# One layer of a hybrid mixer, attention and MLP trunk on one core: the mixer's output projection by seven block products, its convolution by three filters, and the memory values placed behind the projection

## The chip, the core and the metric

The kernel runs on one core of a Trainium2 chip. Five engines take part, each with its own queue of instructions: TensorE (PE; its weight loads, PEld, are listed apart), VectorE (DVE), ScalarE (ACT), GpSimd (POOL), and SyncE (SP), which issues all DMA transfers here. The metric is the device time of one execution in microseconds, as a median of several runs.

## What is computed

One layer, x of 1024 positions by 1024 channels in f32, with three sub-layers, each added to x after an RMS norm:

```python
h = rms_norm(x, pre_mix_g); z = h @ w_in + b_in
y_a = pool_mixer(z[:, :256], pool_w, pool_scale)         # trailing-window means
y_b = spatial_gating_mixer(z[:, 256:1024], ...)          # gMLP on blocks of 128 positions
y_c = conformer_conv_mixer(z[:, 1024:], ...)             # GLU, causal conv of 31 taps, LayerNorm, swish
x = x + rms_norm(concat(y_a, y_b, y_c) @ w_out, post_mix_g)
h = rms_norm(x, pre_x_g); m = rms_norm(mem, mem_g)
x = x + rms_norm(memory_cross_attention(h, m, wq, wk, wv, wo), post_x_g)   # 4 heads, 256 memory tokens
h = rms_norm(x, pre_ff_g)
x = x + rms_norm(square(relu(h @ w_ff1)) @ w_ff2, post_ff_g)               # 4096 hidden
```

The convolution is depthwise over 384 channels: `h = conv(a * sigmoid(g)) + conv_b`, then a LayerNorm over the 384 channels of a position, then swish.

## The kernel before

**Products.** An f32 factor is split into a high part in fp32r (`...h`, a cast on ACT) and a low part (`...l`, source less high part, on DVE or POOL). A product of two such factors is three matmuls (`mm3`): high by high, high by low, low by high. Activations are held transposed, channels on the 128 partitions. `seven` (line 955) multiplies two 1024x1024 matrices by seven products of 512x512 blocks instead of eight; each product has four row blocks of four steps of three matmuls. `left_factors` and `right_factors` make its block sums, in tiles of 1024 columns, and their high and low parts. The query projection (pq), the attention's output projection (ox) and both MLP products go by seven blocks already; the mixer's output projection (omp, lines 978 to 995) goes by plain products: eight blocks of 128 positions by two halves of 512 columns, by eight steps of three matmuls. Behind each block `residual` adds it to x and norms it, and PE transposes the result (om0t to om7t) for pq.

**Stages.** Input norm and the products of the convolution's columns (zg, za) give hc, three tiles of 128 channels by 1024 positions. `conv_taps` (line 588) runs 31 taps for each of three tiles and two halves on DVE, each tap an operation of up to 512 columns on an accumulator in PSUM (cacc). Meanwhile PE runs the products of the other columns (zb), block by block, with the gMLP (zz, vl, sv, ybt) and the pooling (zat, ph, pya) behind them, then the memory's transposes (memt), the keys' product (wkp) and the keys' transposes (kt). `conv_norm` (line 604) goes block by block: PE transposes it to positions on partitions (cnat), DVE takes statistics (cst, cmv), POOL a power of -0.5 (cr...r), DVE scales (cn), PE transposes back (cback), ACT takes the sigmoid (csg). The first half's stands ahead of the values' product (wvp, `mem_product("wv")`), the second half's behind it. Keys and values are then parked in DRAM, and the projection follows.

**What sets the order.** `Schedule` records every operation in the order of the program, and `order` (line 229) then places them by list scheduling: it takes the operation with the earliest planned start on any engine, ties by due time, with planned durations (`_cost`, line 203; a transfer counts at 360 GB/s), planned delays between engines, 49 places of 4 KB per partition for tiles and eight banks of PSUM. Due times come from the order in which the program lists the PE operations. A transfer may be issued at most 150 PE operations ahead of its place. All is fixed before the kernel runs: each engine takes its list in order, and waits where an input is late. Every instruction is recorded under one line, 161, so the names of tiles tell them apart.

Of the kernel before, what the change touches and what calls it, by code (L numbers as in the profile page):

```python
# [10 lines left out]
F32 = mybir.dt.float32  # L11
F32R = mybir.dt.float32r
AF = mybir.ActivationFunctionType
ALU = mybir.AluOpType
# [15 lines left out]
NS = 49  # L30
# [35 lines left out]
class Schedule:  # L66
# [15 lines left out]
    SLACK = 50000.0  # L82
    BYDUE = ("act", "dve", "pool", "sync")
# [119 lines left out]
    def _cost(eng, method, args, kw, ins):  # L203
# [3 lines left out]
        if method == "dma_start":  # L207
            return max(450.0, n * args[0].shape[0] * 4 / 360.0)
# [20 lines left out]
    def order(self):  # L229
        ops, tiles, tags = self.ops, self.tiles, self.tags  # L230
        for i, op in enumerate(ops):
# [5 lines left out]
        due, at = [0.0] * len(ops), 0.0  # L237
        for i, op in enumerate(ops):
            if op.eng == "pe":
                at += op.cost  # L240
            due[i] = at + (0.0 if op.eng == "pe" else self.SLACK)
# [128 lines left out]
def block_kernel(ctx: ExitStack, tc: tile.TileContext, x, mem, pre_mix_g, w_in, b_in, pool_w,  # L370
# [22 lines left out]
    def small(name, n, bufs=24):  # L393
        return sc.tile(mp, [P, n], F32, f"m{n}", bufs, name)
# [93 lines left out]
    for k in range(NK):  # L488
        units[f"out{k}"] = row_unit(f"out{k}", w_out, k)
# [70 lines left out]
    hc = [slot(f"hc{j}", [S]) for j in range(3)]  # L560
    for j, hf in ((0, 0), (1, 0), (0, 1), (1, 1), (2, 0), (2, 1)):
# [15 lines left out]
        else:  # L577
# [4 lines left out]
        dve.scalar_tensor_tensor(hc[j][:, hf * H:(hf + 1) * H], pa, bC[:, j:j + 1], sg,  # L582
                                 ALU.add, ALU.mult)


    yt = [[None] * NK, [None] * NK]

    def conv_taps(hf):
        accs = []
        for j in range(3):  # L590
            acc = bank(f"cacc{hf}{j}")
            dve.tensor_scalar(acc, hc[j][:, hf * H:(hf + 1) * H], cw[:, TAPS - 1, j:j + 1],
                              cb[:, j:j + 1], ALU.mult, ALU.add)
            for s in range(1, TAPS):
                k = TAPS - 1 - s
                a0 = s if hf == 0 else 0
                dve.scalar_tensor_tensor(acc[:, a0:H], hc[j][:, hf * H + a0 - s:hf * H + H - s],
                                         cw[:, k, j:j + 1], acc[:, a0:H], ALU.mult, ALU.add)
            cs = slot(f"cs{hf}{j}", [H])
            act.copy(cs, acc)  # L600
            accs.append(cs)
        return accs

    def conv_norm(hf, cs):
        for j in range(3):
            yt[hf][5 + j] = slot(f"yc{hf}{j}", [2, H], F32R)
        back = [bank(f"cback{hf}{j}") for j in range(3)]
        nat = [bank(f"cnat{hf}{i}") for i in range(2)]
        for b in range(4):
            ps = nat[b % 2]  # L610
            for j in range(3):
                pe.transpose(ps[:, j * P:(j + 1) * P], cs[j][:, b * P:(b + 1) * P], ident)
            st = small(f"cst{hf}{b}", 6)
            dve.bn_stats(st, ps[:, :384])
            mv = small(f"cmv{hf}{b}", 2)
            dve.bn_aggr(mv, st)
            r = rstd_of(f"cr{hf}{b}", mv[:, 1:2], 1)
            nt = slot(f"cn{hf}{b}", [384])
            dve.tensor_scalar(nt, ps[:, :384], mv[:, 0:1], r, ALU.subtract, ALU.mult)
            for j in range(3):  # L620
                pe.transpose(back[j][:, b * P:(b + 1) * P], nt[:, j * P:(j + 1) * P], ident)
        for j in range(3):
            sg = slot(f"csg{hf}{j}", [2, H])
            act.activation(sg[:, 0, :], back[j], AF.Sigmoid, scale=clg[:, j:j + 1],
                           bias=clb[:, j:j + 1])
# [770 lines left out]
```

## Time and profile before

| | |
|---|---|
| median of 3 runs | 1198.07 us (1197.9 to 1200.57) |
| the profiled run, and its span | 1196.5 us, 1194.8 us |
| PE busy | 1158.2 us, 97% |
| DVE busy | 875.1 us, 73% |
| ACT busy | 556.2 us, 47% |
| POOL busy | 271.0 us, 23% |
| DMA | 163.11 MB, mean 137 GB/s |

The durations are of one profiled execution. The busy time of PE is that of pipelined matmuls, and a matmul's listed duration includes its time in the pipe: the distance between the starts of two is what one costs. The stages stand in the trace roughly so: input norm to 41 us, convolution's columns and the blocks of the other columns to 192, keys' product to 226, values' product and the mixer's projection with pq to 428, attention to 490, ox to 580, the MLP's first product to 880, its second to 1186.

### The profile page before, as it was taken

The page shows a single profiled execution, that of the slowest core. Times are in us where ns is not written, and L with a number is a line of the kernel's source. Part 1 is how long each engine was busy: PE and PEld are TensorE (multiplying, and loading weights), DVE is VectorE, ACT ScalarE, POOL GpSimd, SP SyncE. Part 2 cuts the span into 40 slices and gives each one's busy share as a digit, 9 for nine tenths or more (in the row PEclk, how much of TensorE's full clock was granted, in tenths as well). Part 3 has the DMA queues.
Part 4 walks back from the last instruction along what each step waited for, and adds up shares of the span by engine and source line. Part 5 has one row for each costly group of instructions (what it writes and reads, how often), then busy time and mean ns, then how long its engine had stood idle before and what let it go on. Part 6 is the DMA issues. An engine that isn't in the chain of part 4 may idle for free.

```text
span 1194.8 us, 14793 instructions
## 1 busy us (share of the span) xinstructions
PE 1158.2 (97%) x5387; PEld 957.9 (80%) x5387; DVE 875.1 (73%) x1234; ACT 556.2 (47%) x973; POOL 271.0 (23%) x260
## 2 busy tenths in 40 slices
PE   7999999999999999999999999999999999999997
PEld 6788877787877898788778878888888888888885
DVE  5899999464459757799996877667589744587736
ACT  6422245734566358749833434333364632435421
POOL 5352458894062403443000000000000000000001
PEclk9999999999999999999999999999999999999999
DMA  8400024652240313126043355444685244443443
GB/s 275 152 1 1 1 91 164 243 207 89 88 159 28 114 53 107 58 101 229 36 159 123 141 192 169 159 149 142 211 301 210 89 141 169 167 168 132 144 156 141
DMA packets 86056, 163.11 MB, mean 137 GB/s; under 512 B 6475, under 2 KB 29919, under 8 KB 85983
## 3 DMA queue, kind: packets, MB, share of 16 engines
q1 hardware_dynamic: 85982, 162.17, 39.1%
q8 instruction: 42, 0.69, 0.2%
q14 instruction: 32, 0.25, 0.1%
HBM read 116.01 MB, written 46.14 MB: 136 GB/s over the span
## 4 chain that ended last, share of the span: by engine, by line
PE 76%; DVE 9%; ACT 6%; DMA 4%; POOL 2%; issue 2%; SPq 1%; DVEq 0%; ACTq 0%; POOLq 0%
PE g L161 25%; PE fx L161 13%; PE fz L161 7%; PE zb L161 5%; PE ox L161 4%; PE omp L161 4%; PE pq L161 4%; PE zg L161 3%; PE za L161 2%; PE fy L161 2%; DVE cacc L161 2%; PE wkp L161 2%; ACT h L161 1%; PE sc L161 1%; ACT junk L161 1%
## 5 line engine op out<-in xcount | busy, mean ns | idle before, releaser
L161 POOL TENSOR_TENSOR fr0r<-fr0e,half 128x1 f32<-128x1 f32 x1 | 0.9, 866 | 590.2 <-DVE fr0e L161 590.2
L161 DVE SCALAR_TENSOR_TENSOR cacc<-hc,taps,cacc 128x512 f32<-128x512 f32 (+14 forms) x180 | 121.0, 738 | 0.2
L161 DVE TENSOR_TENSOR c<-c,fz 128x512 f32<-128x512 f32 x32 | 21.8, 684 | 52.2 <-PE fz L161 34.1
L161 DVE TENSOR_TENSOR acc<-acc,g 128x512 f32<-128x512 f32 x40 | 25.8, 681 | 33.1 <-PE g L161 33.1
L161 ACT COPY c<-fx 128x512 f32<-128x512 f32 x48 | 28.4, 596 | 38.6 <-PE fx L161 29.2
L161 ACT ACTIVATE c<-fx 128x512 f32<-128x512 f32 x16 | 9.6, 598 | 61.0 <-PE fx L161 61.0
L161 ACT CAST w1o<-w1a 128x512 fp32r<-128x512 f32 x32 | 20.3, 638 | 29.4 <-DVE sb L161 7.8
L161 DVE SCALAR_TENSOR_TENSOR c<-c 128x512 f32<-128x512 f32 x48 | 32.5, 684 | 0.3
L161 PE MATMUL sc<-kv,q 128*128 128x256 f32 x192 | 30.3, 291 | 0.0
L161 ACT ACTIVATE junk<-acc 128x512 f32<-128x512 f32 x16 | 10.1, 632 | 40.8 <-DVE acc L161 40.6
L161 PE MATMUL fx<-h3a40h,w1o 128*128 128x512 f32 x64 | 25.4, 397 | 2.2 <-ACT c L161 2.2
L161 PEld LDWEIGHTS sc<-kv,q 128*128 128x128 f32 x192 | 26.0, 190 | 0.9
L161 ACT CAST w1o<-w1c 128x512 fp32r<-128x512 f32 x32 | 19.6, 626 | 14.2 <-PE fz L161 5.3
L161 PE MATMUL o<-pT,kv 128*128 128x512 f32 x96 | 24.9, 394 | 1.4 <-DVE pT L161 1.4
L161 PE MATMUL fx<-h3a60h,w1o 128*128 128x512 f32 x64 | 25.3, 401 | 0.0
L161 PE MATMUL fx<-h3a11h,w1o 128*128 128x512 f32 x64 | 25.2, 393 | 0.0
L161 PE MATMUL fz<-h3a30h,w1o 128*128 128x512 f32 x64 | 25.1, 392 | 0.0
L161 PE MATMUL fy<-h3a21h,w1o 128*128 128x512 f32 x64 | 25.0, 393 | 0.0
L161 PE MATMUL fy<-h3a20h,w1o 128*128 128x512 f32 x64 | 24.9, 390 | 0.0
L161 PE MATMUL fz<-h3a50h,w1o 128*128 128x512 f32 x64 | 24.9, 389 | 0.0
L161 PE MATMUL fx<-h3a41h,w1o 128*128 128x512 f32 x64 | 24.9, 389 | 0.0
L161 PE MATMUL fz<-h3a31h,w1o 128*128 128x512 f32 x64 | 24.9, 389 | 0.0
(1555 smaller groups left out, 3991.5 us busy)
## 6 DMA issues: line engine op xcount, KB each, us to landing
ha<-scr_hid SPq DMA_DIRECT2D x56, 512.0 KB
scr_hid<-c SPq DMA_DIRECT2D x48, 256.0 KB
scr_hid<-sa SPq DMA_DIRECT2D x32, 256.0 KB
scr_hid<-sb SPq DMA_DIRECT2D x32, 256.0 KB
x<-in_x_dram SPq DMA_DIRECT2D x8, 512.0 KB
omx<-in_x_dram SPq DMA_DIRECT2D x8, 512.0 KB
scr_x<-omx SPq DMA_DIRECT2D x8, 512.0 KB
wqb<-in_wq_dram SPq DMA_DIRECT2D x8, 512.0 KB
```

The costliest lines, as they stand in the source:

```text
L161: op.fn = lambda: f(*[put(a) for a in args], **{k: put(v) for k, v in kw.items()})
```

## The change

- **Projection.** `projection` is written once and called for om and for ox. The mixer's projection goes by `seven`: 336 matmuls in place of 384. Its outputs' factors come from `left_factors`, w_out's from `right_factors`, for om both on DVE (ox keeps half of its right factors on POOL). w_out is loaded as 512-column halves (omwb) and no longer as eight rows (out0 to out7) with low parts on POOL. The mixer's outputs y are kept unsplit in f32 (yq), so their low parts (DVE and POOL) go. 12 sums on DVE and 12 copies on ACT take the products.
- **Convolution.** hc is held by even and odd positions, with their sum hs. Three filters (16 even taps, 15 odd, 16 summed) run over 512 columns for each channel tile, both halves of the sequence at once: 141 tap operations in place of 186, and combining operations behind them.
- **Norm.** `conv_norm` goes in pairs of blocks, each block with a bank of its own; csg is 256 wide (24 operations in place of 12). Both halves follow the keys' product at once.
- **Values.** The values' product and the parking stand behind the projection, ahead of pq.
- **POOL** does its 1024-wide differences and low parts in two halves of 512.
- **Planner.** Transfers count at 220 GB/s; six passes are made, each with due times from the PE order of the one before, and the one with the shortest plan is kept; 50 places; 18 small tiles in place of 24.

```diff
-            return max(450.0, n * args[0].shape[0] * 4 / 360.0)
+            return max(450.0, n * args[0].shape[0] * 4 / 220.0)
...
+        for n in range(self.PASSES):
+            out = self._order(pe)
+            self.spans = getattr(self, "spans", []) + [self.span]
+            if best is None or self.span < best[0]:
+                best = (self.span, out, [op.end for op in self.ops],
+                        {k: r["at"] for k, r in self.tiles.items()})
+            pe = [i for i in out if self.ops[i].eng == "pe"]
...
+        for f, src, w, n in (("a", hc[j][:, 0, :], lambda i: cw[:, 30 - 2 * i, j:j + 1], 16),
+                             ("b", hc[j][:, 1, :], lambda i: cw[:, 29 - 2 * i, j:j + 1], 15),
+                             ("c", hs[j], lambda i: cws[:, 15 - i, j:j + 1], 16)):
+            acc = bank(f"cacc{f}{j}")
+            dve.tensor_scalar_mul(acc, src, w(0))
+            for i in range(1, n):
+                dve.scalar_tensor_tensor(acc[:, i:], src[:, :H - i], w(i), acc[:, i:],
+                                         ALU.mult, ALU.add)
+            accs.append(acc)
+        a, b, c = accs
+        ua = slot(f"cua{j}", [H])
+        act.activation(ua, a, AF.Identity, bias=cb[:, j:j + 1])
+        cs = slot(f"cs{j}", [H, 2])
+        act.copy(cs[:, 0:1, 0], ua[:, 0:1])
+        dve.tensor_tensor(cs[:, 1:, 0], ua[:, 1:], b[:, :H - 1], ALU.add)
+        dve.tensor_tensor(ua, ua, b, ALU.add)
+        dve.scalar_tensor_tensor(cs[:, :, 1], c, cb2[:, j:j + 1], ua, ALU.add, ALU.subtract)
...
+        for pr in range(2):
+            back = [bank(f"cback{hf}{pr}{j}")[:, :256 * n].rearrange("p (j n) -> p j n", n=256)
+                    for j, n in ((0, 2), (1, 1))]
+            for i in range(2):
+                b = pr * 2 + i
+                ps = bank(f"cnat{hf}{b}")
...
+    cs = [conv_taps(j) for j in range(3)]
+    conv_norm(0, cs)
+    conv_norm(1, cs)
...
+        for c in range(2) if eng is pool else (slice(0, 2),):
+            lo_of(eng, lo[:, c], src[:, c], hi[:, c])
...
+            if i == 1:
+                act.copy(row[b][:, c0], ps)
+            elif i == 2:
+                dve.tensor_tensor(row[b][:, c0], row[b][:, c0], ps, ALU.add)
...
+        seven(name, left_factors(name, A), right_factors(f"{name}w", w, (dve, dve) if name == "om" else (pool, dve)), take)
...
+    h2 = projection("om", {hf: [yq[hf][0:2], yq[hf][2:4]] for hf in range(2)}, w_out, g_x,
+                    post_mix_g, x, x1d)
+
+    ps = mem_product("wv")
```

Three places in the orders show what moved. The numbers behind a name tell instances of it apart. First PE behind the keys' transposes (kt), where blocks of the convolution go through their norm; before:

```order
L161 MATMUL cnat00_239<-ident_74,cs00_1429 128x128
L161 MATMUL cnat01_240<-ident_74,cs00_1429 128x128
L161 MATMUL cback02_238<-ident_74,cn00_2565 128x128
L161 MATMUL cnat00_239<-ident_74,cs01_1452 128x128
L161 MATMUL cback02_238<-ident_74,cn01_2573 128x128
L161 MATMUL cnat00_239<-ident_74,cs02_1742 128x128
L161 MATMUL cnat01_240<-ident_74,cs01_1452 128x128
L161 MATMUL wvp00_257<-wv0h_2322,mT00_2259 128x512
L161 MATMUL cnat01_240<-ident_74,cs02_1742 128x128
L161 MATMUL wvp00_257<-wv0l_2571,mT00_2259 128x512
```

and now, the last twelve rows ahead of the projection's second matmul:

```order
L162 MATMUL cnat13_286<-ident_74,cs1_1725 128x128
L162 MATMUL cnat13_286<-ident_74,cs2_1760 128x128
L162 MATMUL cback010_255<-ident_74,cn02_2600 128x128 x2
L162 MATMUL cback010_255<-ident_74,cn03_2613 128x128 x2
L162 MATMUL cback011_256<-ident_74,cn02_2600 128x128
L162 MATMUL cback011_256<-ident_74,cn03_2613 128x128
L162 MATMUL cback100_267<-ident_74,cn10_2629 128x128 x2
L162 MATMUL cback101_268<-ident_74,cn10_2629 128x128
L162 MATMUL cback100_267<-ident_74,cn11_2633 128x128
L162 MATMUL cback101_268<-ident_74,cn11_2633 128x128
L162 MATMUL cback100_267<-ident_74,cn11_2633 128x128
L162 MATMUL om10_291<-omww10h_2355,oma10h_2141 128x512
```

Before, the values' matmuls (wvp) stand among the transposes of the norm; now six blocks (cnat02 to cnat13, 18 transposes) and 16 cback transposes stand between the last kt and the first om10, with no product among them.

DVE at the same place, now: the start of the norm of these six blocks, with parts of the projection's factors (oma, omww) and of the keys (kT01) among them.

```order
L162 BN_STATS cst02_258<-cnat02_257 128x6
L162 BN_STATS cst03_263<-cnat03_262 128x6
L162 BN_AGGR cmv02_259<-cst02_258 128x2
L162 TENSOR_TENSOR oma11l_2579<-yq01_1678,oma11h_1938 128x1024
L162 TENSOR_SCALAR cr02e_260<-cmv02_259 128x1
L162 BN_AGGR cmv03_264<-cst03_263 128x2
L162 TENSOR_TENSOR omww20l_2584<-omwb100_2455,omww20h_2483 128x1024
L162 TENSOR_SCALAR cr03e_265<-cmv03_264 128x1
L162 TENSOR_TENSOR kT01_2591<-kt0_230,kT00_2539 128x512
L162 TENSOR_SCALAR cn02_2600<-cnat02_257,cmv02_259,cr02r_261 128x384
L162 BN_STATS cst10_270<-cnat10_269 128x6
L162 BN_STATS cst11_275<-cnat11_274 128x6
```

The chain from cnat to cn has factor parts of 1024 columns in its way, which were no part of the program before; the second half of a2 (oma21l) stands 43 rows behind the first of these, that of a6 (oma61l) 61.

Last, DVE at the start of the MLP's first product, where the left factors of h3 are made (h3a60l is the low part of the first half of factor 6); before:

```order
L161 TENSOR_TENSOR h3a60l_5619<-h3s20_5595,h3a60h_5607 128x1024
L161 TENSOR_TENSOR h3100_5431<-h3000_5165,h3100_5431 128x1024
L161 TENSOR_TENSOR h3a61l_5638<-h3s21_5604,h3a61h_5623 128x1024
L161 TENSOR_TENSOR h3a50l_5649<-h3s10_5575,h3a50h_5591 128x1024
L161 TENSOR_TENSOR w1o05_5562<-w1a0_5238,w1o05_5562 128x512
L161 TENSOR_TENSOR w1b0_5308<-w1d0_5323,w1b0_5308 128x1024
L161 TENSOR_TENSOR h3101_5443<-h3001_5170,h3101_5443 128x1024
L161 TENSOR_TENSOR w1c0_5256<-w1c0_5256,w1t0_5564 128x1024
L161 TENSOR_TENSOR h3a51l_5685<-h3s11_5586,h3a51h_5599 128x1024
L161 TENSOR_TENSOR w1o07_5679<-w1b0_5308,w1o07_5679 128x512
L161 TENSOR_TENSOR h3010_5188<-h3010_5188,h3s20_5595 128x1024
L161 TENSOR_TENSOR h3011_5234<-h3011_5234,h3s21_5604 128x1024
```

and now:

```order
L162 TENSOR_TENSOR h3a60l_5688<-h3s20_5662,h3a60h_5678 128x1024
L162 TENSOR_TENSOR h3a61l_5697<-h3s21_5673,h3a61h_5685 128x1024
L162 TENSOR_TENSOR w1o16_5665<-w1t0_5629,w1o16_5665 128x512
L162 TENSOR_TENSOR oxh100_5509<-oxh000_5239,oxh100_5509 128x1024
L162 TENSOR_TENSOR w1b0_5421<-w1d0_5445,w1b0_5421 128x1024
L162 TENSOR_TENSOR oxh101_5527<-oxh001_5258,oxh101_5527 128x1024
L162 TENSOR_TENSOR h3a70l_5741<-oxh100_5509,h3a70h_5727 128x1024
L162 TENSOR_TENSOR w1o07_5734<-w1b0_5421,w1o07_5734 128x512
L162 TENSOR_TENSOR w1o17_5738<-w1b0_5421,w1o17_5738 128x512
L162 TENSOR_TENSOR w1o05_5651<-w1a0_5318,w1o05_5651 128x512
L162 TENSOR_TENSOR h3a50l_5766<-h3s10_5640,h3a50h_5657 128x1024
```

h3a70l, the low part of the first half of factor 7, stood fourteenth from h3a60l (two rows behind the last one shown); now it is seventh, and factor 5 comes behind it. (The tiles h3... of before are called oxh... now.)

## Rows read from the trace of the kernel before

**Rows 1.** The page's busy time of each engine, with its share of the span and the number of its instructions.

```profile
PE 1158.2 (97%) x5387; PEld 957.9 (80%) x5387; DVE 875.1 (73%) x1234; ACT 556.2 (47%) x973; POOL 271.0 (23%) x260
```

**Rows 2.** Busy time of each engine by stretch. Columns: the stretch, its length, then PE, PEld, DVE, ACT and POOL busy with the count of instructions, the granted clock of PE as a share of full speed, the DMA engines' busy share, GB/s.

```profile
0.00:41.00 41.00, 31.28 (x197) 27.36 (x198) 25.59 (x51) 26.91 (x47) 22.09 (x62) 1.00 0.79 267
...
140.00:192.00 52.00, 48.56 (x238) 39.25 (x237) 49.70 (x103) 24.05 (x43) 33.24 (x37) 0.98 0.34 122
192.00:226.00 34.00, 31.07 (x146) 25.16 (x147) 25.05 (x47) 20.78 (x32) 26.70 (x25) 0.92 0.40 140
226.00:428.00 202.00, 199.13 (x929) 163.92 (x928) 118.90 (x146) 101.60 (x200) 97.97 (x69) 1.00 0.34 120
428.00:490.00 62.00, 59.28 (x381) 52.93 (x380) 48.38 (x91) 48.00 (x114) 15.64 (x6) 1.00 0.23 77
490.00:580.00 90.00, 89.98 (x428) 74.13 (x427) 78.22 (x102) 65.56 (x155) 33.42 (x21) 1.00 0.40 141
580.00:612.00 32.00, 27.93 (x114) 22.07 (x113) 31.59 (x34) 18.02 (x26) 0.00 (x0) 0.95 0.15 49
612.00:880.00 268.00, 265.85 (x1168) 218.28 (x1167) 193.36 (x281) 105.50 (x175) 0.00 (x0) 1.00 0.48 168
880.00:1186.00 306.00, 306.00 (x1351) 253.11 (x1349) 202.95 (x212) 119.73 (x146) 4.77 (x6) 1.00 0.47 163
```

**Rows 3.** Two pieces of the chain of waits that ended last: start, duration, engine, what, number of instructions.

```profile
489.92 50.83 PE ox L161 x224
...
885.55 300.35 PE g L161 x1325
```

**Rows 4.** What PE waited for, over the whole span: the waiting tile, the engine and tile waited for, us in total, times, the longest.

```profile
PE fx L161 <- DVE h3a70l L161: 3.2, 1, 3.2
PE ybt L161 <- DVE zz L161: 2.9, 2, 2.4
PE fx L161 <- ACT c L161: 2.4, 3, 1.5
PE zat L161 <- ACT zt L161: 2.1, 1, 2.1
PE om6t L161 <- DVE omt L161: 1.5, 1, 1.5
PE o L161 <- DVE pT L161: 1.4, 1, 1.4
...
PE pT L161 <- DVE pt L161: 1.3, 1, 1.3
```

**Rows 5.** The stretches before and behind 600 us, for the tiles omp alone; columns are PE, PEld, DVE and ACT, then clock, DMA share and GB/s.

```profile
0.00:600.00 600.00, 91.10 (x384) 71.29 (x384) 10.86 (x16) 10.85 (x32) 0.99 0.32 109
```

**Rows 6.** The convolution's taps in the page's list of groups: busy us and mean ns of one behind the bar.

```profile
L161 DVE SCALAR_TENSOR_TENSOR cacc<-hc,taps,cacc 128x512 f32<-128x512 f32 (+14 forms) x180 | 121.0, 738 | 0.2
```

**Rows 7.** The timeline of DVE in the query projection: start, duration, what. Two low parts of 1024 columns, one behind the other.

```profile
371.39 1.22 DVE L161 TENSOR_TENSOR h2a60l<-h2s,h2a60h 128x1024 fp32r<-128x1024 f32 x1
372.53 1.22 DVE L161 TENSOR_TENSOR h2a61l<-h2s,h2a61h 128x1024 fp32r<-128x1024 f32 x1
```

**Rows 8.** The timeline of DVE behind the keys' product, in the norm of blocks 2 and 3 of the first half (two statistics in one row).

```profile
227.36 1.02 DVE L161 BATCH_NORM_STATS2 cst<-cnat 128x6 f32<-128x384 f32 x2
...
228.38 0.65 DVE L161 TENSOR_TENSOR kT<-kt,kT 128x512 fp32r<-128x512 f32 x1
...
229.76 0.68 DVE L161 TENSOR_SCALAR cn<-cnat,cmv,cr02r 128x384 f32<-128x384 f32 x1 [0.39 <-POOL cr02r L161]
230.35 0.67 DVE L161 TENSOR_SCALAR cn<-cnat,cmv,cr03r 128x384 f32<-128x384 f32 x1
```

**Rows 9.** The timeline of POOL there: the power for block 2.

```profile
229.17 0.55 POOL L161 TENSOR_TENSOR cr02r<-cr02e,half 128x1 f32<-128x1 f32 x1 [0.78 <-DVE cmv L161]
```

**Rows 10.** The timeline of PE there: ten transposes of the keys, and the three transposes back of block 3.

```profile
223.92 1.26 PE L161 MATMUL kt<-ident,kn 128*128 128x128 f32 x10
...
231.33 0.49 PE L161 MATMUL cback<-ident,cn 128*128 128x128 f32 x3
```

**Rows 11.** The timeline of PE some 12 us earlier: a wait of 2.39 us, and two matmuls that follow each other 3 us later.

```profile
212.00 0.41 PE L161 MATMUL ybt<-ident,zz 128*128 128x128 f32 x2 [2.39 <-DVE zz L161]
...
215.26 0.63 PE L161 MATMUL pya<-ph,pw 128*128 128x512 f32 x1
215.68 0.63 PE L161 MATMUL wkp<-wk6h,mT 128*128 128x512 f32 x1
```

**Rows 12.** The timeline of POOL there: the low parts of the keys' last row of weights.

```profile
217.13 2.58 POOL L161 TENSOR_TENSOR wk7l<-wk7r,wk7h 128x512 fp32r<-128x512 f32 x2
```

**Rows 13.** The timeline of DVE in the attention: the scalings of two pairs of blocks.

```profile
469.06 0.61 DVE L161 TENSOR_SCALAR pt<-pt,rs 128x256 f32<-128x256 f32 x2
...
474.70 3.89 DVE L161 TENSOR_SCALAR pt<-pt,rs 128x256 f32<-128x256 f32 x2
```

**Rows 14.** The timeline of POOL there.

```profile
473.57 2.40 POOL L161 TENSOR_TENSOR wob<-wob,wob 128x1024 f32<-128x1024 f32 x1
476.06 2.38 POOL L161 TENSOR_TENSOR wot<-wob,wob 128x1024 f32<-128x1024 f32 x1
```

**Rows 15.** The timeline of DVE at the start of the MLP's first product: the first and the last of the fourteen instructions shown of the order above.

```profile
584.78 1.22 DVE L161 TENSOR_TENSOR h3a60l<-h3s,h3a60h 128x1024 fp32r<-128x1024 f32 x1
...
597.94 1.21 DVE L161 TENSOR_TENSOR h3a70l<-h,h3a70h 128x1024 fp32r<-128x1024 f32 x1
```

More of the change, by code (lines that the diff above doesn't have):

```diff
@@ L229, in order, with _order @@
     def order(self):
+        best, pe = None, [i for i, op in enumerate(self.ops) if op.eng == "pe"]
+        for n in range(self.PASSES):
[5 more added lines that the diff above has]
+            pe = [i for i in out if self.ops[i].eng == "pe"]
+        self.span, out, ends, places = best
+        for op, end in zip(self.ops, ends):
+            op.end = end
+        for k, at in places.items():
+            self.tiles[k]["at"] = at
+        return out
+    def _order(self, pe_order):
         ops, tiles, tags = self.ops, self.tiles, self.tags
+        for op in ops:
+            op.users = []
         for i, op in enumerate(ops):
@@ L234, in order @@
                 ops[d].users.append(i)
-        due, at = [0.0] * len(ops), 0.0
+        for tag in tags.values():
+            tag["free"] = [(0.0, i) for i in range(tag["bufs"])]
+        for r in tiles.values():
+            r.update(left=len(r["ops"]), end=0.0, live=False, at=0)
+        due, at = [None] * len(ops), 0.0
+        for i in pe_order:
+            at += ops[i].cost
+            due[i] = at
+        at = 0.0
         for i, op in enumerate(ops):
             if op.eng == "pe":
-                at += op.cost
-            due[i] = at + (0.0 if op.eng == "pe" else self.SLACK)
+                at = max(at, due[i])
+            else:
+                due[i] = at + self.SLACK
         for i in range(len(ops) - 1, -1, -1):
@@ L391, in bank, with small @@
         return sc.tile(pp, [P, 512], F32, "b", 8, name)
-    def small(name, n, bufs=24):
+    def small(name, n, bufs=18):
         return sc.tile(mp, [P, n], F32, f"m{n}", bufs, name)
@@ L557, in prod_t @@
                 act_h[k][:, 1, c0:c1], k == 0, k == NK - 1)
-    hc = [slot(f"hc{j}", [S]) for j in range(3)]
+    hc = [slot(f"hc{j}", [2, H]) for j in range(3)]
+    hs = [slot(f"hs{j}", [H]) for j in range(3)]
     for j, hf in ((0, 0), (1, 0), (0, 1), (1, 1), (2, 0), (2, 1)):
@@ L604, in conv_norm @@
-    def conv_norm(hf, cs):
[L605 to L610, printed above, removed]
-            for j in range(3):
[L612 to L625, printed above, removed]
-            act.activation(sg[:, 1, :], back[j], AF.Identity, scale=clg[:, j:j + 1],
-                           bias=clb[:, j:j + 1])
-            dve.tensor_tensor(sg[:, 1, :], sg[:, 1, :], sg[:, 0, :], ALU.mult)
-            y = yt[hf][5 + j]
-            act.copy(y[:, 0, :], sg[:, 1, :])
-            lo_of(pool, y[:, 1, :], sg[:, 1, :], y[:, 0, :])
@@ new lines, in block_kernel, with y_of @@
+        dve.tensor_tensor(hs[j][:, c], hc[j][:, 0, c], hc[j][:, 1, c], ALU.add)
+    yq = [[slot(f"yq{hf}{t}", [2, H]) for t in range(4)] for hf in range(2)]
+    def y_of(hf, i):
+        return yq[hf][i // 2][:, i % 2, :]
+    cws = sc.tile(cp, [P, 16, 3], F32, "cws", 1, "cws")
+    dve.tensor_copy(cws[:, 0, :], cw[:, 0, :])
+    dve.tensor_tensor(cws[:, 1:16, :], cw[:, 2:TAPS:2, :], cw[:, 1:TAPS - 1:2, :], ALU.add)
+    cb2 = sc.tile(cp, [P, 3], F32, "cb2", 1, "cb2")
+    dve.tensor_scalar(cb2, cb, 2.0, None, ALU.mult)
@@ L710, in block_kernel @@
             zaT[hf][m] = slot(f"zaT{hf}{m}", [H + 16])
-        for j in range(3):
-            yt[hf][2 + j] = slot(f"yb{hf}{j}", [2, H], F32R)
         for pr in range(2):
@@ L933, in sub @@
             for e in range(2):
[L934 removed]
+                for c in range(2) if eng[e] is pool else (slice(0, 2),):
+                    eng[e].tensor_tensor(o[e][:, c], x[e][:, c], y[e][:, c], ALU.subtract)
         def factor(i):
```

156 lines of the change are left out of this document (67 added, 89 removed).

## The prediction

> **What bounds the kernel now.** I read the busy time of the engines first: TensorE (PE) is busy for 1158.2 of 1194.8 us, and VectorE (DVE) for 875.1 [rows 1]. The table of stretches then shows where PE is not busy [rows 2]: the idle time from 140 to 1186 us is 3.4, 2.9, 2.9, 2.7, 0, 4.1 and 2.2 us by stretch (length less PE's busy time), some 18 us in all; the rest lies in the first 41 us (9.7), which the change hardly touches, and in the last nine. The granted clock is below 1.00 in three of these stretches, and costs at most 0.08 x 34 = 2.7, 0.02 x 52 = 1.0 and 0.05 x 32 = 1.6 us there. In the chain of waits, PE's products run end to end: 224 matmuls in 50.83 us, 1325 in 300.35 us, 0.227 us for each at full clock [rows 3]. So a matmul less is 0.227 us less, and beside that there are some 18 us of idle time and 5 us of clock to win, each with a name in the list of PE's waits [rows 4].
>
> [...]
>
> **The change part by part.** The profiled run took 1196.5 us, 1.6 below the median of 1198.07; the sum is made against it.
>
> 1. The projection's matmuls: 384 now [rows 5], seven products of 4 x 4 x 3 = 336 then; 48 x 0.227 = **-10.9**.
>
> 2. The convolution's normalisation. PE has, so far, matmuls of the values' product to do while a block goes through statistics, power, scaling and back (the order of before shows them interleaved, and the trace shows wvp running with the last two blocks). The values' product is now behind the projection, and the order of after has nothing for PE between the last key transpose and the first om10 but 18 cnat and 16 cback transposes: 34 x 0.109 = 3.7 us [rows 10]. What releases them is DVE: six statistics at 0.47, six aggregates and six small sums (some 0.6 together), four scalings at 0.59, one kT part of 0.6 [rows 8] and the two 1024-wide lo parts that the order puts among them at 1.14 [rows 7], 8.7 us; a power on GpSimd, 0.55 [rows 9], is partly exposed, and the first statistics and the last transposes add 1.5. That is 10.8 us from the last kt to om10, less 3.7 of transposes: 7.1 us of new idle time. After such a wait the clock falls: behind the wait of 2.39 us for zz the matmuls stood 0.42 us apart [rows 11], so I add 1. Bounds: if the blocks interlock better than I count, +3; if the three remaining pairs run one after another (one pair took 4.5 us from its statistics at 227.36 to the last cback at 231.82 [rows 8, 10], so 3 x 4.5, with 3 x 0.65 of transposes ahead and 4 x 1.14 of lo parts between, 20.0 less 3.7) it is 16.3, with 2.7 of clock **+19**. Taken **+8**, nearest to the rows of one pair counted out singly.
>
> 3. The factors of the projection. Left and right factors each add 22 operations of 1024 columns on DVE, 44 x 1.14 = 50 us [rows 7], and 14 casts each on ACT, beside 336 x 0.227 = 76 us of PE. In the stretch from 226 to 428 us DVE was busy for 118.9 of 202 us [rows 2], so there is room in the sum. But they bunch: the first three products (36 us of PE) want a1, a2, a6 and w1, w2, w6, and some of the norm stands ahead of them. By the order, the second half of a2 is some 20 us of DVE work behind the start of the norm and that of a6 some 38 us; PE is there, after the stall of term 2, at about 23 and 37 us. About level: **+1**, bounds 0 and +6 (five 1024-wide operations late).
>
> 4. Behind the projection the values' product (96 matmuls, 22 us) now covers the last blocks' residuals. The wait of om6t for omt, 1.5 us [rows 4], was the largest part of the 2.9 us idle between 226 and 428 us [rows 2]; in the order of after wvp rows lie among om4t to om7t. **-2**, bounds -2.9 and 0. What parks keys and values goes later by as much and has all of pq (76 us) before it is read back.
>
> 5. From 140 to 226 us: 6.4 us idle and up to 3.7 of clock [rows 2], by name ybt for zz (2.9) and zat for zt (2.1) [rows 4]. The convolution loses a quarter of its taps: 186 to 141, at 121.0 / 180 = 0.67 us [rows 6] -30 us, with some +7 for nine combining operations of 512 columns at 0.6 [rows 8] and six sums of half the width, all on DVE, which was busy for 49.7 of 52 us here. Against that, GpSimd sets the end of the keys' product (wk7l is done at 219.7 [rows 12], its matmuls run behind it), and the order puts four pya and six ybt behind sv with no keys' matmuls between, where four stood before. GpSimd's work in this place stays. **-1.5**, bounds -5 and +2.
>
> 6. From 428 to 490 us: 2.7 us idle, o for pT and pT for pt, 1.4 and 1.3 [rows 4]. Two scalings of pt took 3.89 us where two others took 0.61 [rows 13], while GpSimd ran two 1024-wide operations of 2.4 us [rows 14]. These are now halves of 512, so such a hold shortens to about half. The Trainium skill ("SBUF — State Buffer", Who interferes with whom) says that GpSimd's only port is DVE's second one, held for a whole instruction; the 3.89 us agree. **-1.5**, bounds -2.7 and 0.
>
> 7. From 580 to 612 us: 4.1 idle, of them 3.2 for h3a70l [rows 4], and 1.6 of clock. DVE was busy without a gap, and h3a70l stood last of fourteen [rows 15]; now it is seventh, ahead of h3a50l and h3a51l, and PE takes the products in that order. **-2.5**, bounds -5 and +1.
>
> 8. From 612 to 880 us: 2.2 idle [rows 2], fx for c 2.4 in three waits [rows 4]; loads planned at 220 GB/s, and six passes, may move a DMA-bound wait. **-1**, bounds -2.2 and +1.
>
> Sum: -10.9 + 8 + 1 - 2 - 1.5 - 1.5 - 2.5 - 1 = **-10.4**; 1186.1 us for a profiled run, 1187.7 for the median. Terms 4 to 8 are -8.5 together. DVE in all: 875 - 23 + 50 + 7 (12 sums of 512 columns that take the products, at 0.6), less the lo parts of y that go, about 905 us: still well below PE.
>
> **The rivals.**
>
> A, slower: the pairs of the norm run one after another through the eight PSUM banks (four hold kt, until DVE splits the last two far behind the norm), term 2 is +19, and the factors, which stand behind the same DVE work, come 6 us late. 1198.1 - 10.9 + 25 - 8.5 = **1203.7**. It decides above 23 us of new idle time (10.9 + 8.5 + 3.6). For it: kt2 and kt3 are split behind the norm in DVE's order. Against it: the order alternates blocks, and cr00 and cr01 are done before kt. The Trainium skill ("Perfetto Trace Analysis", Optimization Strategy) takes a repeated gap for a want of buffers for the next tile; no row of before shows that here, since wvp covered the norm.
>
> B, no measurable change: the new order keeps as many waits as it removes, since each pass of the planner moves all of them (terms 4 to 8 nothing). 1198.1 - 10.9 + 8 + 1 = **1196.2**. For it: the waits are short and scattered, and an order planned by fixed durations cannot see a port hold of 3.89 us. Against it: h3a70l's and om6t's causes are removed by rows.
>
> C, more: the norm's stall is +3, the factors cost nothing, and terms 4 to 8 come half way to their lower bounds (-13.2). 1198.1 - 10.9 + 3 - 13.2 = **1177.0**. For it: DVE is lighter by 23 us ahead of 226 us, and loads planned slower are issued earlier.
>
> D, the change does not do what it says: seven products with one of their inputs late give back the 48 matmuls by waits inside the projection. That is term 3 at its bound or beyond it, and would end between B and A.
>
> **How the numbers follow.** Forecast 0.55 (its own range 1181 to 1194), A with D's worse part 0.10, B 0.15, C 0.20. A measurement of this kernel can tell some 0.3% from no change, 3.6 us: 1194.5 to 1201.7. So faster 0.75, same 0.15, slower 0.10. The range goes from 1179 to 1197: it leaves out A and half of C.
>
> **What would show it.** In the profile after: some 336 matmuls om1 to om7 at 0.227 us; a stretch of about 11 us behind the last kt in which PE is under half busy with cnat and cback, and a fall of the granted clock at its end (term 2); om's waits for omw or oma parts by DVE of 1 us or none (3); no wait of om6t for omt (4); no pt scaling of 3 us or more (6); no 3 us wait for h3a70l (7). The prediction is wrong if the stall behind kt is above 15 or below 4 us, if the projection waits inside its products for DVE by more than 6 us, or if new waits of several us stand in stretches that had none, 41 to 140, 490 to 580 and the second layer product from 880 us, where nothing was to be won.

## The result, and the profile after

The changed kernel takes 1182.50 us (median; 1182.12 to 1183.73), beside 1197.99 of the kernel before (four runs now) on the same chips: ratio 0.9874, 95% interval 0.9848 to 0.99, some 12 to 18 us less. The profiled run took 1183.7 us, 12.8 below that of before. Forecast was 1187.7; the time lies in the range and in the forecast's own range. By the medians the gain, 15.5 us, is half as large again as the 10.4 us of the sum; the account by stretches below is of the 12.8 us between the two profiled runs.

The page's busy time answers to [rows 1]: 48 matmuls fewer, PE busy for 9.3 us less, DVE for 39 us more.

```profile
PE 1148.9 (97%) x5339; PEld 951.0 (80%) x5339; DVE 914.2 (77%) x1253; ACT 578.8 (49%) x1011; POOL 260.0 (22%) x260
```

The stretches, to be read beside [rows 2] (columns as there). The cuts are at about the same work: the last kt is done at 223.5, and the 16.5 us behind it are the norm.

```profile
0.00:41.00 41.00, 32.20 (x200) 27.92 (x201) 26.36 (x51) 26.76 (x47) 18.55 (x57) 1.00 0.74 249
41.00:140.00 99.00, 97.87 (x444) 80.08 (x443) 85.10 (x150) 24.56 (x42) 37.27 (x37) 1.00 0.09 27
140.00:186.00 46.00, 46.00 (x224) 37.98 (x224) 43.50 (x88) 18.55 (x32) 29.74 (x36) 1.00 0.29 104
186.00:223.50 37.50, 33.32 (x164) 27.27 (x163) 19.06 (x37) 19.72 (x35) 29.14 (x27) 0.91 0.39 141
223.50:240.00 16.50, 11.33 (x53) 8.77 (x52) 13.95 (x35) 13.96 (x26) 4.37 (x6) 0.69 0.00 0
240.00:300.00 60.00, 60.00 (x274) 49.88 (x273) 57.21 (x70) 38.12 (x65) 6.81 (x7) 1.00 0.30 102
300.00:346.00 46.00, 44.66 (x217) 36.13 (x216) 33.36 (x40) 39.48 (x100) 33.54 (x27) 1.00 0.68 245
346.00:391.00 45.00, 42.25 (x182) 33.41 (x181) 39.89 (x29) 25.45 (x35) 30.33 (x16) 1.00 0.32 120
...
425.00:484.00 59.00, 58.17 (x377) 51.96 (x377) 45.25 (x91) 46.43 (x112) 11.07 (x9) 1.00 0.24 81
...
570.00:600.00 30.00, 29.83 (x139) 24.25 (x138) 29.43 (x34) 24.18 (x51) 1.62 (x2) 1.00 0.11 36
600.00:868.00 268.00, 268.00 (x1182) 221.16 (x1182) 200.66 (x291) 104.42 (x176) 0.00 (x0) 1.00 0.48 168
868.00:1174.00 306.00, 305.25 (x1347) 252.43 (x1345) 203.25 (x214) 122.65 (x149) 4.84 (x6) 1.00 0.48 166
```

Idle time (length less PE's busy time) is now 0.2 us in the start of the MLP, where it was 4.1, nothing in the rest of the MLP's first product (2.2), 0.8 in the attention (2.7) and 4.2 ahead of the keys' end (6.4). Against that stand 5.2 us at 0.69 of the clock behind the keys, where there was next to none, 4.1 us between 300 and 391 (2.9 for the whole stretch before), 1.1 us ahead of 140, and 0.8 us in the MLP's second product from 868 us, where there was none.

What PE waited for, to be read beside [rows 4]: no h3a70l, no om6t; new are cnat for kT, and pq for the factors of h2.

```profile
PE cnat L162 <- DVE kT L162: 4.2, 1, 4.2
PE ybt L162 <- DVE zz L162: 2.7, 2, 2.0
...
PE pq L162 <- ACT h2a61h L162: 1.6, 1, 1.6
...
PE pT L162 <- DVE pt L162: 0.8, 1, 0.8
PE pq L162 <- DVE wqw61l L162: 0.8, 1, 0.8
```

The timeline of PE behind the last kt: the first om10 starts at 235.98, 12.4 us behind the last kt's end, and the om matmuls then stand 0.43 us apart for a while, which is the lower of the clock's two levels.

```profile
223.96 0.82 PE L162 MATMUL cnat<-ident,cs 128*128 128x128 f32 x6
228.99 2.79 PE L162 MATMUL cnat<-ident,cs 128*128 128x128 f32 x12 [4.22 <-DVE kT L162]
...
233.60 1.25 PE L162 MATMUL cback<-ident,cn 128*128 128x128 f32 x4 [0.61 <-DVE cn L162]
235.07 1.11 PE L162 MATMUL cback<-ident,cn 128*128 128x128 f32 x4 [0.22 <-ACT csg L162]
235.98 0.80 PE L162 MATMUL om<-omww10h,oma10h 128*128 128x512 f32 x1
236.57 0.63 PE L162 MATMUL om<-omww10l,oma10h 128*128 128x512 f32 x1
237.00 0.63 PE L162 MATMUL om<-omww10h,oma10l 128*128 128x512 f32 x1
```

DVE at the same time: the twelve cnat wait for a bank of PSUM that DVE empties with the kT at 228.16, which stands behind two statistics and two 1024-wide low parts of the projection's factors. From 224.70 us until past the first om10 DVE itself was idle only once, for 0.47 us. Ahead of all this it had been idle for 11.84 us, since its next instruction waited for the power cr00r, on POOL behind wk7l.

```profile
217.19 0.68 DVE L162 TENSOR_SCALAR cn<-cnat,cmv,cr00r 128x384 f32<-128x384 f32 x1 [11.84 <-POOL cr00r L162]
...
224.70 1.03 DVE L162 BATCH_NORM_STATS2 cst<-cnat 128x6 f32<-128x384 f32 x2 [2.85 <-PE cnat L162]
...
225.73 1.19 DVE L162 TENSOR_TENSOR oma11l<-yq,oma11h 128x1024 fp32r<-128x1024 f32 x1
...
226.99 1.19 DVE L162 TENSOR_TENSOR omww20l<-omwb,omww20h 128x1024 fp32r<-128x1024 f32 x1
...
228.16 0.68 DVE L162 TENSOR_TENSOR kT<-kt,kT 128x512 fp32r<-128x512 f32 x1
```

### The profile page after: what moved, and what is told of

The parts are those of the page before. It is cut to its first block, busy times and chain, and to the rows that moved or that the text cites. A ratio compares the mean times of both kernels' runs of the same rounds, so it can differ in the third digit from the quotient of the medians.

```text
span 1181.7 us, 14682 instructions
## 1 busy us (share of the span) xinstructions
PE 1148.9 (97%) x5339; PEld 951.0 (80%) x5339; DVE 914.2 (77%) x1253; ACT 578.8 (49%) x1011; POOL 260.0 (22%) x260
## 4 chain that ended last, share of the span: by engine, by line
PE 86%; DVE 8%; ACT 3%; issue 1%; POOL 1%; DMA 1%; DVEq 0%; POOLq 0%; ACTq 0%
PE g L162 26%; PE fx L162 14%; PE fz L162 7%; PE om L162 6%; PE pq L162 6%; PE ox L162 6%; PE zb L162 5%; PE fy L162 3%; PE zg L162 2%; PE za L162 2%; DVE cacca L162 2%; PE wkp L162 2%; PE o L162 2%; PE sc L162 2%; ACT junk L162 1%
## 5 line engine op out<-in xcount | busy, mean ns | idle before, releaser
L162 DVE SCALAR_TENSOR_TENSOR cacca<-hc,taps,cacca 128x511 f32<-128x511 f32 (+14 forms) x45 | 32.7, 755 | 0.0
L162 DVE SCALAR_TENSOR_TENSOR caccc<-hs,cws,caccc 128x511 f32<-128x511 f32 (+14 forms) x45 | 32.1, 747 | 0.0
L162 DVE SCALAR_TENSOR_TENSOR caccb<-hc,taps,caccb 128x511 f32<-128x511 f32 (+13 forms) x42 | 30.8, 750 | 0.1
L162 PE MATMUL fz<-h3a51h,w1o 128*128 128x512 f32 x64 | 24.9, 389 | 0.0
L162 PE MATMUL fx<-h3a70h,w1o 128*128 128x512 f32 x64 | 24.9, 391 | 0.0
```

The lines of the kernel that those rows point to most:

```text
L162: op.fn = lambda: f(*[put(a) for a in args], **{k: put(v) for k, v in kw.items()})
```

## The experiments

Ratios are to the kernel before, with 95% intervals; the changed kernel stands at 0.9874. The table cuts each profiled run at the same work: where the first matmul of the attention (sc), of the MLP's first product (fx) and of its second (g) starts. The second product and what follows it took 321.9 to 323.3 us in every run.

| us | up to the attention | attention and ox | MLP's first product |
|---|---|---|---|
| before | 426.7 | 134.6 | 310.6 |
| changed | 425.3 | 132.0 | 302.6 |
| e3_plan_only | 420.7 | 138.5 | 306.4 |
| e5_old_plan | 440.6 | 136.7 | 314.8 |
| e11_one_pass | 434.2 | 135.3 | 312.0 |
| e4_proj_only | 431.4 | 132.8 | 306.6 |
| e6_proj_plan | 433.9 | 136.6 | 303.5 |
| e1_wv_back | 427.4 | 137.5 | 301.5 |
| e2_norm_first | 448.1 | 131.8 | 303.4 |
| e12_norm_half_first | 437.7 | 132.0 | 301.9 |
| e7_conv_undone | 426.4 | 132.0 | 302.6 |
| e8_whole_pool | 430.0 | 137.0 | 304.7 |
| e9_whole_same_order | 428.4 | 133.4 | 302.6 |

Of the 13.1 us by which the changed kernel's span is shorter, 8.0 lie in the MLP's first product, and 1.4 ahead of the attention, where the projection, the convolution, the norm and the values stand.

### The planner

**e3_plan_only.** The kernel before with the new planner:

```diff
-            return max(450.0, n * args[0].shape[0] * 4 / 360.0)
+            return max(450.0, n * args[0].shape[0] * 4 / 220.0)
...
+        for n in range(self.PASSES):
+            out = self._order(pe)
```

> The kernel before with nothing but the planner's two changes: transfers at 220 GB/s and six passes. Theory (the waits that left between 428 and 880 us, some 9 us, left by the new order): 1188 to 1191 us, with the wait for h3a70l under 1.5 us. Rival (they left because DVE and GpSimd have less to do or shorter holds): 1195 to 1199 us, with that wait at 2 to 4 us.

Measured: 1189.52 us, 0.9939 (0.9924 to 0.9954). The time is the theory's, and the wait for h3a70l is gone, but the gain does not stand where the theory put it:

```profile
PE pT L162 <- DVE pt L162: 3.3, 2, 2.0
...
PE fx L162 <- ACT c L162: 1.8, 2, 1.0
PE om6t L162 <- DVE omt L162: 1.4, 1, 1.4
PE fx L162 <- DVE h3a71l L162: 1.3, 1, 1.3
```

By the table 6.0 of the 6.6 us of span are won ahead of the attention. From there to the MLP's second product, where the theory had its 9 us, the sum is what it was (444.9 and 445.2 us): the MLP's first product is 4.2 us shorter, attention and ox are 3.9 longer. The wait of pT is longer than before, and in the MLP's start h3a71l, h3a61l and c have come up where h3a70l stood: idle is 3.9 us there (576 to 606 us), as good as the 4.1 of before, and what left is the fall of the clock and the idle time behind it. So the theory's time came out right by luck.

**e5_old_plan** is the changed kernel with 360 GB/s and one pass, **e11_one_pass** with 220 GB/s and one pass:

```diff
-    PASSES = 6
+    PASSES = 1
```

> The changed kernel under the old planner: transfers at 360 GB/s, one pass. Theory (the plan is worth the same 8 us here as it was by itself): 1189 to 1192 us. Rival (the factors of the projection crowd DVE, as the projection by itself showed with some 10 us of new waits, and only the new plan sets them in time): 1194 us or more, with waits of om and pq for DVE of 5 us or more together.

> The changed kernel with one pass of the planner, transfers still at 220 GB/s. With 360 GB/s and one pass it took 1214.8. Theory (the due times from the PE order of an earlier pass are what matters): 1206 us or more. Rival (the rate for the transfers is what matters, the passes choose among near equals): 1183 to 1192 us.

Measured: 1214.77 us, 1.0143 (1.0128 to 1.0158), and 1205.55, 1.0072 (1.0052 to 1.0093). The rival of the first holds by its time, the theory of the second but for half a microsecond, which is within its spread: without its planner the changed kernel is slower than the one before. Of the 32 us the rate is worth 9 with one pass, and the five further passes 23 at the new rate; six passes at the old rate were not run. The longest waits of e5_old_plan stand where the projection's results, the norm and the MLP's factors are made:

```profile
PE om2t L162 <- DVE omt L162: 7.3, 1, 7.3
...
PE cnat L162 <- ACT csg L162: 4.5, 1, 4.5
PE fx L162 <- DVE w1o L162: 4.2, 1, 4.2
```

The waits that the rival named, of om and pq for the factors, were not it (0.3 us of pq for wqw61l); the longest is for omt, the norm of the projection's blocks.

### The projection by seven products

**e4_proj_only** is the kernel before with `projection` for om, y in f32, and nothing else; **e6_proj_plan** the same under the new planner.

```diff
-            for n, i in steps:
-                wh, wl = W(f"out{i}")
...
+    h2 = projection("om", {hf: [yq[hf][0:2], yq[hf][2:4]] for hf in range(2)}, w_out, g_x,
+                    post_mix_g, x, x1d)
```

> The kernel before with the projection by seven products and nothing else (31 taps, values' product ahead of the projection, old planner, GpSimd operations whole; it has 50 places for tiles). Theory (48 matmuls are worth 0.227 us each wherever they stand, and the factors cost PE no wait): -10 to -11, 1187 to 1188 us. Rival (the gain of the whole change was made by the order, and the factors make PE wait under the old plan): 1192 us or more. The wait for h3a70l should stay at some 3 us, since DVE's order there is the old one.

> The kernel before with the projection by seven products and the new planner, and nothing else: 31 taps, values' product ahead of the projection, GpSimd operations whole. Theory (the plan takes its 8 us, and the factors' waits stay, since DVE paces the stretch of norm, values and factors): 1186 to 1190 us; what is left to 1182.5 is the lighter convolution's and the values' place. Rival (the plan alone removes the factors' waits): 1178 to 1183 us.

Measured: 1196.16 us, 0.9997 (0.9986 to 1.0007), and 1198.56, 1.0017 (1.0003 to 1.0032). Both theories and the second rival fell; the first rival holds (1192 or more). The 48 matmuls are gone, and their 10.9 us are given back by new waits: up to the attention e4_proj_only takes 4.7 us more than before. The wait for h3a70l, expected to stay at some 3 us, is half of that, and the MLP's first product is 4.0 us shorter. Of the projection alone:

```profile
PE cback L161 <- DVE vm L161: 3.5, 1, 3.5
PE pq L161 <- DVE wqw61l L161: 2.6, 1, 2.6
PE pq L161 <- DVE omb4e L161: 1.8, 1, 1.8
PE om6t L161 <- ACT omh L161: 1.7, 1, 1.7
PE fx L161 <- DVE h3a70l L161: 1.5, 1, 1.5
```

The longest, cback for vm, stands in the norm. Three more, 6.1 us together, stand at the end of the projection: seven products give the last four blocks all at once, in the last product, and pq follows at once and wants h2. This is rival D's outcome, though that rival had the waits inside the projection: there om waits only 1.2 us, for omr. The new planner does not help (e6_proj_plan: vm 3.8, pq for h2a11l 3.1, wqw61l 2.6, om6t for omh 2.3). In the changed kernel the values' product stands between the projection and pq; what that is worth, the next run tells.

### The values' product and the norm

**e1_wv_back** puts the values' product back between the norm's halves:

```diff
     conv_norm(0, cs)
+    ps = mem_product("wv")
...
     conv_norm(1, cs)
```

> The changed kernel with the values' product put back between the two halves of the convolution's norm, as it stood before; the parking stays behind the projection. Theory (the 9 us between the last kt and om10 are a norm without cover): the wait of cnat for kT, 4.2 us, and the half clock behind it go, -7 to -9; the start of pq loses its cover and gives 1 to 3 back. 1174 to 1178 us. Rival (DVE, not the missing products, sets the pace there, since norm and factors share it): the wait moves into the projection's first products or to the end of the values' product, 1180 to 1184 us.

Measured: 1192.69 us, 0.997 (0.9959 to 0.9981), 10 us slower than the changed kernel; theory and rival both fell by size. The wait of cnat for kT is gone, as the theory has it. In its place, and in the attention:

```profile
PE pT L162 <- DVE pt L162: 3.0, 4, 0.8
...
PE om L162 <- DVE vm L162: 2.4, 1, 2.4
...
PE om L162 <- DVE cmv L162: 2.2, 1, 2.2
PE om L162 <- DVE omww50l L162: 1.8, 1, 1.8
PE pq L162 <- DVE h2a60l L162: 1.6, 1, 1.6
```

The norm's second half now stands uncovered ahead of om (cmv), the second product waits for the banks of the values' product until DVE has emptied them (vm), and pq waits for h2 behind a projection with nothing after it.

By stage, with the 96 matmuls of the values' product (21.8 us) taken off on both sides: the last kt to the first om takes some 6 us less than in the changed kernel (222.9 to 250.4 us here, 223.4 to 236.0 there), as the theory had it, and the first om to the attention some 9 us more (250.4 to 427.4 and 236.0 to 425.3), where it had 1 to 3. The place is thus worth 2 to 3 us; a further 5.5 of the 7.4 us of span stand in attention and ox, with PE's wait of pT for pt at 3.0 us in place of 0.8. The edit touches nothing there; the plan that came with it does.

**e10_wv_back_cheap** asks if DVE's load is the cause. It has e1_wv_back's order on every engine, but 28 low parts are zeroed (so this part of the projection is left out):

```diff
+        if name.startswith("om") and eng is dve:
+            lo_of(eng, lo, src, hi)
+            sc.ops[-1].fn = lambda: nc.vector.memset(sc.put(lo).bitcast(F32), 0.0)
+            return hi, lo
```

> The kernel with the values' product put back, with every engine's order as it was there, but the 28 low parts of the projection's factors are set to zero on DVE in place of being computed (that part of the product is left out). Theory (DVE paces norm, values and factors there, so that the wait which left the keys came back inside the projection): the om waits of 2.4, 2.2 and 1.8 us shrink, 1192.7 falls to 1181 to 1186 us. Rival (those waits have other causes: banks, POOL's powers, ACT): 1189 us or more.

Measured: 1192.14 us, 0.9959 (0.9947 to 0.9971): no difference, in the rival's range, and the three waits of om are 2.4, 2.2 and 1.7 us still. By itself this tells little on DVE's load: a zeroing of 1024 columns held DVE nearly as long as a low part by itself does (1.07 us apart, and 1.14 [rows 7]). Only the first four low parts were much lighter: in e1_wv_back they stood beside low parts of POOL and took twice as long. Two of them in e1_wv_back, then the same two and the norm's statistics here:

```profile
238.57 2.32 DVE L162 TENSOR_TENSOR oma10l<-yq,oma10h 128x1024 fp32r<-128x1024 f32 x1
240.81 2.31 DVE L162 TENSOR_TENSOR omww11l<-omwb,omww11h 128x1024 fp32r<-128x1024 f32 x1
```

```profile
239.11 0.91 DVE L928 MEMSET oma10l<- 128x1024 f32 x1 [0.16 <-issue]
240.18 0.91 DVE L928 MEMSET omww11l<- 128x1024 f32 x1 [0.16 <-POOL wv6l L162]
...
248.50 1.11 DVE L162 BATCH_NORM_STATS2 cst<-cnat 128x6 f32<-128x384 f32 x2 [5.28 <-PE cnat L162]
```

Yet the wait for cmv did not move, and DVE had been idle for 5.28 us just ahead of it, until PE gave it the blocks (cnat). So that wait is no lack of DVE time. How much of the other two is load stays open.

**e2_norm_first** writes convolution and both halves of the norm ahead of the keys' product, **e12_norm_half_first** the first half only:

```diff
+    cs = [conv_taps(j) for j in range(3)]
+    conv_norm(0, cs)
     ps = mem_product("wk")
```

> The changed kernel with convolution and norm written ahead of the keys' product, so that this may cover the norm. Theory (missing cover): no stall between kt and om10, 1174 to 1178 us if the keys' product covers the norm. Rival (in the order all cnat stand ahead of sv and ybt, and most of the keys' product behind the norm): the same wait stands ahead of the keys' product, and joins the waits for sv and ybt there: 1181 to 1186 us.

> The changed kernel with the convolution and the first half's norm written ahead of the keys' product, the second half's behind it. Theory (the keys' product covers half of the norm, and DVE, idle for 12 us there, has the time): the stall behind the last kt falls by 3 to 6 us: 1176 to 1180 us. Rival (banks and ACT's sigmoid, which PE then waits for ahead of the keys' product, take it back, as with both halves ahead): 1184 us or more.

Measured: 1206.89 us, 1.0084 (1.0069 to 1.0099), and 1194.48, 0.9976 (0.9964 to 0.9988): both rivals by sign; the first time is far above its rival's range, the second in it (1184 or more). Of e12_norm_half_first:

```profile
PE sv L162 <- ACT vh L162: 7.4, 1, 7.4
...
PE sv L162 <- DVE zp L162: 2.7, 1, 2.7
PE om L162 <- DVE cmv L162: 2.6, 1, 2.6
```

The largest stands at 112 us, far ahead of the norm: PE's order there has sv directly behind zat, where the changed kernel's has dozens of zb products between the two, so PE waits out the whole chain to vh. The norm has no part in it; it came with the new plan. The wait of om for cmv is the uncovered second half.

The stall itself did shrink, as the theory of e12_norm_half_first has it: from the last kt to the first pq it took 104.7 us (244.0 to 348.7), and the changed kernel 110.1 (223.4 to 333.5); some 2 to 3 of these 5.4 us are transposes that moved ahead. But the last kt came 20.6 us later. So the norm's place gave something back, and the order ahead of it took more; how much of that the place forces and how much is the plan's choice, these runs don't separate.

### The convolution

**e7_conv_undone** is the changed kernel with 31 taps for each tile and half:

```diff
-        for f, src, w, n in (("a", hc[j][:, 0, :], lambda i: cw[:, 30 - 2 * i, j:j + 1], 16),
...
+            for s in range(1, TAPS):
+                k = TAPS - 1 - s
```

> The changed kernel with the convolution as it was, 31 taps for each tile and half. Theory (the taps lie beside PE's work up to 185 us, and what they free is idle on DVE, 12 us of it ahead of the norm): 1182 to 1185 us. Rival (DVE paces the norm and the projection's start, and some 23 us more of work before that delay it): 1189 us or more.

Measured: 1185.07 us, 0.9902 (0.9883 to 0.992): the theory's time. Three filters come with 2 to 3 us here, though they take a quarter of the taps off DVE. Where the convolution runs they show no gain: with 31 taps the last kt came at 220.3 us, 3.1 earlier than in the changed kernel, and that lead was lost behind it, ahead of pq (which starts at 338.2 us there, at 333.5 in the changed kernel), in an order planned anew. They were not tried by themselves on the kernel before, nor with the order held.

### GpSimd's halves

**e8_whole_pool** undoes the halves; **e9_whole_same_order** does each pair as one operation where its first half stood, with the changed kernel's order on every engine:

```diff
-        for c in range(2) if eng is pool else (slice(0, 2),):
-            lo_of(eng, lo[:, c], src[:, c], hi[:, c])
+        lo_of(eng, lo, src, hi)
```

> The changed kernel with GpSimd's 1024-wide operations whole again. Theory (halves shorten the holds of DVE in the attention, up to 2 us): 1183 to 1185 us, with a scaling of pt above 2 us. Rival (the new plan sets them apart anyway): within 1 us of 1182.5.

> The changed kernel with every engine's order as it is, but each pair of GpSimd halves done as one operation of 1024 columns where the first half stood. It tells the length of GpSimd's operations from the new plan that came with it in the run before. Theory (the holds themselves cost the time): 1191 to 1196 us, with a pt scaling of 2 us or more. Rival (the plan for whole operations was the worse one, the holds cost little): 1182 to 1185 us.

Measured: 1196.1 us, 0.9988 (0.9978 to 0.9997), and 1188.59, 0.9929 (0.9914 to 0.9945). Theory and rival of the first both fell by size: the halves are worth 13.6 us. The second lies between its two answers: some 6 us are the longer operations themselves, some 7.5 the other order that the planner makes of them. The scalings of pt, to be read beside [rows 13], in ns as least, median and most, in the kernel before, the changed one, e8_whole_pool and e9_whole_same_order:

```profile
L161 DVE TENSOR_SCALAR pt<-pt,rs x32: 334/349/2540, 434.1 to 481.9; 128x256 f32<-128x256 f32 x32
L162 DVE TENSOR_SCALAR pt<-pt,rs x32: 333/349/1435, 432.6 to 477.4; 128x256 f32<-128x256 f32 x32
L162 DVE TENSOR_SCALAR pt<-pt,rs x32: 335/349/2498, 437.3 to 484.6; 128x256 f32<-128x256 f32 x32
L172 DVE TENSOR_SCALAR pt<-pt,rs x32: 332/349/2489, 435.8 to 481.6; 128x256 f32<-128x256 f32 x32
```

The longest is 2.5 us where GpSimd's operations are whole (2.4 us each [rows 14]) and 1.4 where they are halves. PE's wait of pT for pt is 3.1 us in e8_whole_pool, 1.8 in e9_whole_same_order and 0.8 in the changed kernel. But by the table e9_whole_same_order loses 1.4 us in attention and ox, and 3.1 ahead of them, where PE's waits of pq are 5.3 us together (2.7 in the changed kernel), most of them for low parts.

## Why the prediction held

The sign, the forecast and the range held, and seven of eight terms had the right sign or came to nothing. That the sum came so near is in part luck: up to the attention (terms 1 to 5) it had -5.4 and the table of the experiments shows -1.4; in the MLP (terms 7 and 8) it had -3.5, and the table shows -8.0. Two misses of 4 us and more cancel. By term, against the profiled run of before:

| term | forecast | measured | from |
|---|---|---|---|
| 1 matmuls | -10.9 | -10.9 | 48 fewer, 0.227 each |
| 2 norm | +8 | +9.5 | 12.4 us less 3.7 of transposes, and some 0.8 of om at half clock |
| 3 factors | +1 | 0 | no idle time from 240 to 300 us |
| 4 projection's end | -2 | +1.2 | idle 2.9 then, 4.1 from 300 to 391 us |
| 5 140 to 226 us | -1.5 | -1.4 | idle 6.4 to 4.2, clock 3.7 to 3.4, 1.1 idle ahead of 140 us |
| 6 attention | -1.5 | -1.9 | idle 2.7 to 0.8 |
| 7 MLP's start | -2.5 | -5.5 | idle 4.1 to 0.2, clock 1.6 to 0 |
| 8 MLP's first product | -1 | -2.2 | idle 2.2 to 0 |

With 0.9 us less idle time in the first 41 us the measured terms make -12.1, beside -12.8 of the profiled run. Term 1 was not measured by itself: 48 matmuls are gone, and 0.227 us each is the spacing of the others.

**Term 2** was the best founded: its 10.8 us from kt to om10 were 12.4. Its working, a queue of DVE's instructions one behind the other, is what the rows show: DVE is idle for only 0.47 us of it. PE meets that queue at rival A's link, though: it waits 4.2 us for a bank that kt holds until DVE splits it. The rival's price was the wrong part; there was one such wait and not one for each pair. Inside the term two sizes were off and partly cancel: 7.1 us of idle time were forecast and 5.2 measured, and 1 us for the clock, where it cost some 4 (0.69 over 16.5 us), since the transposes too ran at the lower level: the twelve behind the wait took 2.8 us, and 1.3 at 0.109 each.

**Term 4** failed in sign. The step was "the values' product now covers the last blocks' residuals": it does, and om6t's wait is gone, but the blocks come later and all together, and pq meets ACT and DVE still at h2a61h and wqw61l. The saving was counted and its next in line was not named. What the term gives back is small beside what the values' product holds off, which the sum did not contain: with it put back, some 9 us more stand between the first om and the attention (e1_wv_back, less some 6 won in the norm), and a projection by itself earns nothing (e4_proj_only).

**Terms 7 and 8** were under-sized. h3a70l stands 6.3 us behind h3a60l now (581.6 and 587.9 us) and 13.2 before [rows 15], so the wait could go as a whole, and with it the fall of the clock. I had halved it for doubt. It is not the new order of the two low parts alone: the MLP's first product takes 306.4 us with the plan alone, 306.6 with the projection alone, 312.0 and 314.8 with all of the change and one pass, and 301.5 to 304.7 in every run that has the new projection and six passes. What in those plans does it is open.

**Term 6**'s mechanism is shown by e8_whole_pool and e9_whole_same_order: the longest scaling of pt falls from 2.5 to 1.4 us, about half, as the working has it. But the halves are worth far more than the attention's 1.9 us: some 6 with the order held, and 13.6 with the order that a planner makes for whole operations. The Trainium skill's rule cited there ("SBUF — State Buffer", Who interferes with whom) agrees. Two runs with one order bear on it as well: DVE's low parts took 2.3 us beside POOL's in e1_wv_back, and zeroings in their place, which read nothing, 0.91 in e10_wv_back_cheap.

**The sum as a method** did less well than its result. I took 48 matmuls as -10.9 that stand by themselves and the rest as small corrections. The experiments show parts that don't add: against the kernel before in the same round, the projection alone -1 (within its interval nothing), with the planner +1, the planner alone -7.7, and all of it without the planner +17. The order carries most of the gain. Rival B's doubt (a new order keeps as many waits as it removes) was wrong for this change and right for others that were planned by the same six passes, the projection alone among them. One reason that it gave is not so: the planner does allow for a port hold. `order`, before and after, keeps a time `port` for DVE and for POOL, and plans an operation that needs it behind the other engine's. So whole operations are planned with longer holds, and e8_whole_pool gets another order. Why six passes found an order without the 7.3 us wait for omt and one pass did not is open.

## What to carry to other kernels

Fewer matmuls on a full TensorE pay only if what stands behind the shortened stage is ready as early: block products give their last results together, so independent products between them and their reader are worth a try; here they were worth some 9 us behind the projection and cost some 6 where they had covered the norm. Where a list scheduler sets the order, no part of a change has a price of its own: time it with the order held (one operation's length changed, every engine's order kept) and with the order planned anew, and count the difference as the plan's. Compare two such runs stage by stage, cut at the same work: a total that fits a theory (e3_plan_only) or a loss that seems to belong to the edit (e1_wv_back) can stand in another stage. Look for who empties a PSUM bank before asking who fills it: the wait of 4.2 us was for a low part queued behind unrelated work.

## What was not expected of the hardware

A zeroing of 128x1024 f32 on DVE took 0.91 us and stood 1.07 us from the next instruction, little less than a subtraction of two such tiles (1.14 us apart). Beside subtractions of POOL the same subtraction took 2.3 us, and POOL's were slowed too: a pair of 128x512 took 3.5 and 4.5 us there, and 2.6 beside zeroings (e1_wv_back and e10_wv_back_cheap). And with no instruction moved on any other engine, GpSimd operations of 1024 columns in place of two of 512 cost 6 us over the whole kernel, though GpSimd is busy for 22% of it.
